# Weights split ahead of their stage get buffers and a schedule of their own, and the first norm's gain moves from the weights to the rows

## The chip, the cores and the metric

The kernel runs on one core of a Trainium2 chip. The time is device microseconds of one execution; a lower one is better. All figures of the trace come from one profiled execution of the kernel before.

## What is computed

Two layers on 512 rows of 1024 values, all float32. The first, a gated short convolution, is the part that the change touches:

```python
h = rmsnorm(x, a_norm)                      # (512, 1024)
b, c, u, z = split(h @ a_w_in, 4)           # a_w_in is 1024 x 8192: 64 column tiles of 128
conv = causal 3-tap convolution of c * u    # per column
x = x + (b * conv * silu(z)) @ a_w_out      # a_w_out is 2048 x 1024
```

Then keys and values are computed from the new x (w_kv, two small compression networks), and an attention layer with three branches follows, whose query, gate and output weights are b_w_in and b_w_out; a last rmsnorm ends it. rmsnorm(x, g) is x times the reciprocal root of its mean square, times the vector g.

## The kernel before

Every product is made in three passes: each float32 operand is split into a high part (rounded to the matmul type) and a low part (the rest), and high x high, high x low and low x high are summed in PSUM (`mm3`, line 160). So every weight tile has to be loaded, rounded on ScalarE (line 148) and subtracted on VectorE (line 149) before TensorE can use it.

Class `Stream` (line 97) does that for a list of units of 128 x 1024 values, in order. `load` (line 108) issues a unit's load on SP's queue into one of NRAW = 3 buffers named raw; `split` (line 122) lets GpSimd multiply it by a norm's gain where it has one (line 147), then makes the high and low tiles. `get(i)` (line 155) hands out unit i, after it has asked for loads up to unit i + 4 and splits up to unit i + 2. A raw buffer is free again when its subtraction has ended. The high and low tiles of the projections have three pairs of buffers (pool `wp`), those of a_w_out four (`wop`).

The list `ws` serves the convolution. Lines 210 to 217 write its order: for each pair of column tiles the eight projection units, and two units of a_w_out among them. For each of the 16 column tiles `conv_tile` (line 304) runs four projections of 24 matmuls with 512 columns (products c, u, z, b), with the convolution and the gate on VectorE and ScalarE (lines 312 to 333). In each pair from the second to the seventh, after its second projection, the four `out_tile` calls (line 336) of the pair before come in a burst: 48 matmuls and eight additions to x on VectorE (line 348). The first norm's gain a_norm is multiplied into each of the 64 units of a_w_in on GpSimd (line 248 passes it, columns S_A of the table `sm`).

24 units of the second layer's weights (q, z and o for four groups) are split ahead in this stage, stored as high and low parts to a tensor in memory (w_dram), and loaded ready from there later (line 125). Lines 220 to 232 mix them into the order of `ws`, about one to every two or three units, so that they use the same three raw buffers; their high and low parts go to four tiles vh0, vl0, vh1 and vl1 in turn, from which line 151 stores them, right behind the split. Before the last two pairs `v_unit` (line 353) loads the weights of V, five raws, through the raw buffers too, and multiplies them by their gains on GpSimd (line 361).

The compiler fixes at compile time in which order each engine, and each queue, issues its instructions: by the order of the program and by when it reckons each one ready. At run time each engine keeps that order and waits on semaphores.

At the start four matmuls on zeros (line 264) run while x arrives. Each of four row tiles is then squared and scaled (`norm_tile`, line 266; the scaling is line 270), transposed (line 181) and split; the first two units of a_w_in are split in quarters, the second one's low part on GpSimd, and their products are made in halves as the row tiles become ready (lines 283 to 294).

Of the kernel before, what the change touches and what calls it, by code (L numbers as in the profile page):

```python
# [9 lines left out]
F32 = mybir.dt.float32  # L10
# [15 lines left out]
S_A = 128  # L26
S_END = 136
# [7 lines left out]
Q0, Z0, Q1, Z1 = 3, 1, 7, 3  # L35

# [6 lines left out]
def trunk_kernel(  # L43
# [13 lines left out]
    small: bass.AP,  # L57
    cst: bass.AP,
# [38 lines left out]
    class Stream:  # L97
# [3 lines left out]
        def add(self, src, a, b, gain=None, pool_=None, tag="w", lo=None, parts=1, put=None):  # L101
            self.units.append((src, a, b, gain, pool_, tag, lo or dve, parts, put))
# [19 lines left out]
        def split(self, upto):  # L122
            while self.at < min(upto, len(self.units)):
# [10 lines left out]
                src, a, b, gain, p_, tag, lo, parts, put = self.units[self.at]  # L134
                r = self.raws[self.at]
                if put is not None:
                    hl_ = p_.tile([128, 2, a, b], F32R, name=tag)
                    h, l = hl_[:, 0], hl_[:, 1]
                else:
                    q = p_ or wp  # L140
                    h = q.tile([128, a, b], F32R, name=tag + "h")
                    l = q.tile([128, a, b], F32R, name=tag + "l")
# [7 lines left out]
                if put is not None:  # L150
                    nc.sync.dma_start(put, f(hl_).rearrange("p s a b -> p s (a b)"))
# [36 lines left out]
    def index_of(order, x_):  # L188
        return order.index(x_)
# [3 lines left out]
    wd = kd.tile([6 * G, 128, 2, 1024], F32, name="w_dram")  # L193
    ready = {}

# [10 lines left out]
    if True:  # L206
# [3 lines left out]
        for i in range(NCT // 2):  # L210
# [12 lines left out]
        first, last_ = index_of(order, ("in", 1, 1)), index_of(order, ("in", 1, 2 * (NCT // 2 - 2)))  # L223
        mixed = []
        n = 0
        for i, o in enumerate(order):
            mixed.append(o)
            while n < len(ahead) and i >= first and (i - first) * len(ahead) >= (n + 1) * (last_ - first - 2):
                mixed.append(("ahead", *ahead[n]))
                n += 1  # L230
        assert n == len(ahead)
        order = mixed
        for o in order:
            index[o] = len(ws.units)
            if o[0] == "ahead":
                kind, g, j = o[1:]
# [131 lines left out]
        for i in range(NCT // 2):  # L368
# [608 lines left out]
```

## Time and profile before

| | |
|---|---|
| median of 3 runs | 880.68 us (876.94 to 881.38) |
| the profiled execution | 880.71 us, of which the span from the first to the last instruction is 878.9 us |
| TensorE, matmuls | 833.6 us busy, 95% of the span |
| TensorE, weight loads | 671.1 us, beside the matmuls |
| VectorE, ScalarE, GpSimd | 612.9, 386.2 and 273.5 us busy |

An engine that is not the bound may be idle without cost; busy time is an average over stages that differ. In the rows below PE is TensorE (PEld its weight loads), DVE VectorE, ACT ScalarE, POOL GpSimd and SP the engine that issues most transfers; L149 is line 149 of the kernel before.

### The profile page before, as it was taken

How to read it: one execution, taken by the hardware profiler on the slowest of the kernel's cores; microseconds unless marked ns; L12 is line 12 of the kernel's file. 1: busy time of each engine (PE TensorE's matmuls, PEld its weight loads, DVE VectorE, ACT ScalarE, POOL GpSimd, SP SyncE). 2: the span in 40 equal slices, each digit the busy share in tenths (PEclk: the TensorE clock that was granted, in tenths of full speed). 3: DMA queues.
4: the chain of work that ended last, by engine and by line, in shares of the span. 5: the costliest groups of instructions: out<-in, count | busy, mean ns of one | idle time of the engine just before them, and what ended most of it. 6: DMA issues, size and time to landing. Idle time of an engine off the chain costs nothing.

```text
span 878.9 us, 10999 instructions
## 1 busy us (share of the span) xinstructions
PE 833.6 (95%) x4004; PEld 671.1 (76%) x4004; DVE 612.9 (70%) x1073; ACT 386.2 (44%) x741; POOL 273.5 (31%) x194
## 2 busy tenths in 40 slices
PE   7999998998999989989999998999999999999995
PEld 6888876776868868868887997776777877877883
DVE  6657646567466485775558529856989869877987
ACT  6422321341243223322233324524867557667675
POOL 6526235334324443443322017220023014012002
PEclk9999999999999999989999999999999999999998
DMA  7477587576486676443352002595214235141212
GB/s 240 116 236 213 180 259 211 166 249 205 145 261 204 193 227 215 136 137 96 96 168 72 1 22 81 170 268 209 85 37 120 66 127 144 49 144 53 93 48 96
DMA packets 121014, 128.31 MB, mean 146 GB/s; under 512 B 5376, under 2 KB 104064, under 8 KB 117888
## 3 DMA queue, kind: packets, MB, share of 16 engines
q1 hardware_dynamic: 117392, 122.50, 44.8%
q0 software_dynamic: 2304, 4.20, 2.2%
q10 hardware_dynamic: 1264, 0.92, 0.3%
q8 instruction: 31, 0.51, 0.2%
q14 instruction: 23, 0.19, 0.1%
HBM read 98.24 MB, written 29.36 MB: 145 GB/s over the span
## 4 chain that ended last, share of the span: by engine, by line
PE 39%; DVE 10%; DMA 4%; ACT 4%; POOL 3%; issue 2%; SPq 0%; ACTq 0%; POOLq 0%; DVEq 0%
PE mm L165 14%; PE mm L690 5%; PE mm L612 4%; PE mm L670 4%; PE pt L774 3%; DVE wl L149 2%; PE o L766 2%; PE o L767 2%; PE s L728 2%; DMA raw<-in_w_kv_dram 2%; PE s L729 2%; DMA raw<-in_a_w_in_dram 1%; POOL raw L147 1%; DVE im L494 1%; ACT wh L148 1%
## 5 line engine op out<-in xcount | busy, mean ns | idle before, releaser
L147 POOL TENSOR_TENSOR raw<-raw,sm 128x1024 f32<-128x1024 f32 (+1 forms) x86 | 169.9, 1985 | 232.4 <-DMA raw<-in_a_w_in_dram 143.1
L165 PE MATMUL mm<-hh,wh 128*128 128x512 f32 (+1 forms) x592 | 233.7, 395 | 7.7 <-DVE x L348 7.5
L165 PE MATMUL mm<-hh,wl 128*128 128x512 f32 (+1 forms) x592 | 232.2, 392 | 3.8 <-DVE wl L149 3.8
L165 PE MATMUL mm<-hl,wh 128*128 128x512 f32 (+1 forms) x592 | 232.7, 393 | 0.4 <-DVE hl L184 0.4
L149 DVE TENSOR_TENSOR wl<-raw,wh 128x1024 fp32r<-128x1024 f32 (+1 forms) x82 | 123.0, 1502 | 38.9 <-ACT wh L148 38.4
L148 ACT ACTIVATE wh<-raw 128x1024 fp32r<-128x1024 f32 (+1 forms) x86 | 85.4, 997 | 141.2 <-PE mm L165 73.2
L165 PEld LDWEIGHTS mm<-hh,wh 128*128 128x128 f32 x592 | 112.5, 190 | 36.0 <-DVE x L348 8.3
L165 PEld LDWEIGHTS mm<-hh,wl 128*128 128x128 f32 x592 | 112.3, 190 | 31.6 <-DVE wl L149 5.6
L165 PEld LDWEIGHTS mm<-hl,wh 128*128 128x128 f32 x592 | 112.6, 190 | 25.4 <-DVE hl L184 0.6
L779 DVE TENSOR_TENSOR pl<-pt,ph 128x512 fp32r<-128x512 f32 x80 | 53.8, 683 | 8.9 <-ACT ph L777 8.0
L165 PE MATMUL mm<-woh,yh 128*128 128x512 f32 x128 | 51.2, 400 | 8.1 <-DVE vp L318 4.6
L777 ACT ACTIVATE ph<-pt 128x512 fp32r<-128x512 f32 x80 | 46.6, 591 | 16.3 <-PE pt L774 14.8
L165 PE MATMUL mm<-woh,yl 128*128 128x512 f32 x128 | 51.1, 399 | 2.5 <-DVE yl L332 2.5
L149 DVE TENSOR_TENSOR vl<-raw,vl 128x1024 fp32r<-128x1024 f32 x12 | 20.0, 1669 | 43.3 <-ACT vl L148 43.3
L165 PE MATMUL mm<-wol,yh 128*128 128x512 f32 x128 | 50.2, 392 | 0.0
L737 ACT ACTIVATE P<-P,st 128x512 f32<-128x512 f32 (+1 forms) x64 | 39.0, 610 | 18.3 <-DVE st L736 18.0
L148 ACT ACTIVATE vl<-raw 128x1024 fp32r<-128x1024 f32 x12 | 12.7, 1061 | 76.3 <-POOL raw L147 39.2
L728 PE MATMUL s<-kh,qs 128*128 128x512 f32 (+3 forms) x128 | 42.1, 341 | 3.7 <-DVE st L736 3.2
L348 DVE TENSOR_TENSOR x<-mm,x 128x512 f32<-128x512 f32 x64 | 41.3, 680 | 5.1 <-PE mm L165 5.1
L774 PE MATMUL pt<-cs,P 128*128 128x128 f32 x192 | 42.4, 275 | 0.0
L729 PE MATMUL s<-kl,qs 128*128 128x512 f32 (+3 forms) x128 | 40.2, 328 | 0.0
L736 DVE CUSTOM_DVE_ANT_0 P<-s,causal 128x512 f32<-128x512 f32 (+1 forms) x64 | 34.6, 550 | 7.4 <-PE s L729 6.7
(206 smaller groups left out, 1608.2 us busy)
## 6 DMA issues: line engine op xcount, KB each, us to landing
raw<-in_a_w_in_dram SPq DMA_DIRECT2D x62, 512.0 KB, 4.8
w_dram<-vh SPq DMA_DIRECT2D x12, 1024.0 KB, 5.1
w_dram<-vl SPq DMA_DIRECT2D x12, 1024.0 KB, 6.2
wh<-w_dram SPq DMA_DIRECT2D x24, 512.0 KB, 4.2
wl<-w_dram SPq DMA_DIRECT2D x24, 512.0 KB, 5.0
raw<-in_b_w_in_dram SPq DMA_DIRECT2D x16, 512.0 KB, 6.7
raw<-in_a_w_out_dram SPq DMA_DIRECT2D x16, 512.0 KB, 3.5
raw<-in_w_kv_dram SPq DMA_DIRECT2D x12, 512.0 KB, 4.5
```

What stands on the lines that cost most here:

```text
L147: pool.tensor_mul(r[:, c], r[:, c], gain[:, c, None].to_broadcast([128, w, b]))
L148: act.activation(h[:, c], r[:, c], AF.Copy)
L149: lo.tensor_sub(l[:, c], r[:, c], f(h[:, c]))
L165: pe.matmul(o, lhsT=a, rhs=b, start=(i == 0), stop=(i == n - 1))
L348: dve.tensor_add(o, p, o)
L690: pe.matmul(p, lhsT=a[:, j, ts_], rhs=b, start=(n == 0), stop=(n == 5))
L728: pe.matmul(p[:, :n], lhsT=q, rhs=K[g][0][:, s, :n], start=True, stop=False)
L729: pe.matmul(p[:, :n], lhsT=q, rhs=K[g][1][:, s, :n], start=False, stop=True)
L737: exps.append(lambda: act.activation(P[:, :n], P[:, :n], AF.Exp, bias=self.st[:, 0, i:i + 1], scale=-1.0, accum_out=self.st[:, 1, i:i + 1]))
L774: pe.transpose(p[:, h, :], self.P[h, s][:, kt * 128:(kt + 1) * 128], ident)
L777: act.activation(ph, p, AF.Copy)
L779: subs.append(lambda p=p, ph=ph, pl=pl: dve.tensor_sub(pl, p, f(ph)))
```

## The change

A class `Ahead` takes the 24 units out of `ws`. A unit is loaded straight into the low half of one of the four tiles (vh0, vl0, vh1, vl1), its high part is made in the other half, and the subtraction is made in place. One `tick` n issues the load of unit n + 2, the split of unit n and the store of unit n - 1. After each of the 64 projection steps the loop asks for as many ticks as the share of steps between the fifth (A0) and the 46th (A1) gives. The units' order becomes q, z, o within each group and half. `ready_or` and `KV_AHEAD = False` leave the units of the stage after as they were.

The units of a_w_in have no gain any more. The vector a_norm is loaded as one row, a product of a column of ones with it spreads it over all 128 rows in two PSUM banks, and the first norm's scaling takes it as a second factor, half a row at a time. Of the four matmuls on zeros one goes.

```diff
-S_A = 128
-S_END = 136
+S_END = 128
...
+A0, A1 = 5, 46
+KV_AHEAD = False
...
-                if put is not None:
-                    hl_ = p_.tile([128, 2, a, b], F32R, name=tag)
-                    h, l = hl_[:, 0], hl_[:, 1]
...
-                if put is not None:
-                    nc.sync.dma_start(put, f(hl_).rearrange("p s a b -> p s (a b)"))
...
+    class Ahead:
+        def __init__(self):
+            self.units, self.slots, self.at, self.out = [], {}, 0, 0
+
+        def add(self, key, src, a, b, gain=None):
+            ready[key] = (wd[len(self.units)], a, b)
+            self.units.append((src, a, b, gain))
+
+        def load(self, n):
+            if n < len(self.units):
+                src, a, b, _ = self.units[n]
+                r = vwp.tile([128, 2, a, b], F32, name=("vh0", "vl0", "vh1", "vl1")[n % 4])
+                nc.sync.dma_start(r[:, 1], src)
+                self.slots[n] = r
+
+        def tick(self):
+
+            n = self.at
+            if n == 0:
+                self.load(0)
+                self.load(1)
+            self.load(n + 2)
+            if n < len(self.units):
+                _, a, b, gain = self.units[n]
+                r = self.slots[n]
+                if gain is not None:
+                    pool.tensor_mul(r[:, 1], r[:, 1], gain[:, :, None].to_broadcast([128, a, b]))
+                act.activation(r[:, 0].bitcast(F32R), r[:, 1], AF.Copy)
+                dve.tensor_sub(r[:, 1].bitcast(F32R), r[:, 1], r[:, 0])
+            if 0 < n <= len(self.units):
+                nc.sync.dma_start(wd[n - 1], self.slots.pop(n - 1).rearrange("p s a b -> p s (a b)"))
+            self.at += 1
+
+        def upto(self, share):
+            while self.at < share * (len(self.units) + 1):
+                self.tick()
...
-        ahead = [("q", 0, 0), ("q", 0, 1)] + [
-            (k, g_, j) for g in range(G) for k, g_ in (("z", g), ("o", g), ("q", g + 1)) if g_ < G for j in range(2)
-        ]
...
-                ws.add(row_units(a_w_in, o[1] * CD + o[2] * 128), KC, 128, sm[:, S_A:S_A + KC], lo=pool if len(ws.units) == 1 else dve, parts=4 if len(ws.units) < 2 else 1)
+            if o[0] == "in":
+                ws.add(row_units(a_w_in, o[1] * CD + o[2] * 128), KC, 128, None, lo=pool if len(ws.units) == 1 else dve, parts=4 if len(ws.units) < 2 else 1)
...
+        grow = wop.tile([1, D], F32, name="woh", padded_shape=[128, D])
+        ones = wop.tile([1, 128], F32, name="wol", padded_shape=[128, D])
+        pool.memset(ones, 1.0)
+        nc.scalar.dma_start(grow, a_norm)
         nc.scalar.dma_start(sm, small)
...
-        for _ in range(4):
+        gain = []
+        for d in range(2):
+            p = psum.tile([128, 512], F32, name="mm")
+            pe.matmul(p, lhsT=ones, rhs=grow[:, d * 512:(d + 1) * 512], start=True, stop=True)
+            gain.append(p)
+        for _ in range(3):
...
-            dve.tensor_scalar(xn, x2[:, t, :], r, None, op0=OP.mult)
+            if gain is None:
+                dve.tensor_scalar(xn, x2[:, t, :], r, None, op0=OP.mult)
+            else:
+                for d in range(2):
+                    c = slice(d * 512, d * 512 + 512)
+                    dve.scalar_tensor_tensor(xn[:, c], x2[:, t, c], r, gain[d], op0=OP.mult, op1=OP.mult)
...
+        for g in range(G):
+            for j in range(2):
+                ah.add(("q", g, j), row_units(b_w_in, g * 256 + j * 128), KC, 128, bq)
+                ah.add(("z", g, j), row_units(b_w_in, 1072 + g * 256 + j * 128), KC, 128, gb)
+                ah.add(("o", g, j), b_w_out[(2 * g + j) * 128:(2 * g + j + 1) * 128, :].rearrange("p (a b) -> p a b", a=1), 1, 1024)
+        seen = 0
         for i in range(NCT // 2):
...
                 for _ in conv_tile(c):
                     n += 1
+                    seen += 1
+                    ah.upto(min(1.0, max(0.0, (seen - A0) / (A1 - A0))))
```

## Rows read from the trace of the kernel before

**Rows 1.** The page: busy us, share of the span and instructions per engine

```profile
PE 833.6 (95%) x4004; PEld 671.1 (76%) x4004; DVE 612.9 (70%) x1073; ACT 386.2 (44%) x741; POOL 273.5 (31%) x194
```

**Rows 2.** Table by stage: length; PE, PEld, DVE, ACT, POOL busy (instructions); clock; DMA; GB/s

```profile
26.50:120.00 93.50, 93.50 (x404) 75.52 (x403) 60.39 (x57) 30.29 (x34) 38.95 (x22) 1.00 0.65 200
120.00:400.00 280.00, 262.85 (x1095) 206.88 (x1095) 178.13 (x173) 84.81 (x96) 116.00 (x65) 0.98 0.65 197
400.00:460.00 60.00, 60.00 (x259) 48.28 (x258) 35.41 (x34) 17.78 (x21) 16.73 (x11) 1.00 0.41 120
```

**Rows 3.** TensorE's waits, 120 to 400 us: total, times, longest

```profile
PE mm L165 <- DVE x L348: 7.5, 5, 2.9
PE mm L165 <- DVE vp L318: 4.6, 3, 2.8
PE mm L165 <- ACT yh L331: 3.4, 4, 1.5
PE mm L165 <- DVE yl L332: 1.6, 3, 0.6
```

**Rows 4.** Chain that ended last, in order of time: start, length, what

```profile
338.81 7.94 DMA raw<-in_a_w_in_dram
...
346.89 1.91 POOL raw L147
...
348.82 1.07 ACT wh L148
...
349.91 2.01 DVE wl L149
```

**Rows 5.** DMA issues, 120 to 400 us: count, KB each, median us to landing

```profile
raw<-in_a_w_in_dram SPq DMA_DIRECT2D x39, 512.0 KB, 4.9
...
w_dram<-vl SPq DMA_DIRECT2D x9, 1024.0 KB, 6.1
raw<-in_b_w_in_dram SPq DMA_DIRECT2D x11, 512.0 KB, 6.7
raw<-in_a_w_out_dram SPq DMA_DIRECT2D x8, 512.0 KB, 3.8
raw<-in_b_w_out_dram SPq DMA_DIRECT2D x6, 512.0 KB, 5.8
```

**Rows 6.** Groups by line, 120 to 400 us: busy us, mean ns, idle before and releasers

```profile
L147 POOL TENSOR_TENSOR raw<-raw,sm 128x1024 f32<-128x1024 f32 x45 | 94.8, 2115 | 124.9 <-DMA raw<-in_a_w_in_dram 91.6 <-DMA raw<-in_b_w_in_dram 22.7 <-DVE cv L322 6.6
...
L149 DVE TENSOR_TENSOR wl<-raw,wh 128x1024 fp32r<-128x1024 f32 x36 | 55.3, 1535 | 23.5 <-ACT wh L148 23.4
...
L149 DVE TENSOR_TENSOR vl<-raw,vl 128x1024 fp32r<-128x1024 f32 x9 | 14.1, 1564 | 38.2 <-ACT vl L148 38.2
...
L318 DVE TENSOR_TENSOR vp<-mm,cc 128x512 f32<-128x512 f32 x9 | 6.1, 681 | 0.4 <-PE mm L165 0.4
```

**Rows 7.** The start: two small loads, timeline rows of TensorE, durations of the norm's scaling

```profile
sm<-in_small_dram ACTq DMA_DIRECT2D x1, 68.0 KB, 5.1
cs<-in_cst_dram ACTq DMA_DIRECT2D x1, 64.0 KB, 4.0
...
1.23 5.49 PE L264 MATMUL mm<-causal 128*128 128x384 f32 x8 [1.23 <-POOL causal L89]
...
7.10 1.09 PE L181 MATMUL mm<-cs,xn 128*128 128x128 f32 x8 [0.38 <-DVE xn L270]
...
14.91 1.94 DVE L270 TENSOR_SCALAR xn<-x,stat 128x1024 f32<-128x1024 f32 x1
...
17.82 0.37 PE L165 MATMUL mm<-hh,wh 128*128 128x256 f32 x1
...
L270 DVE TENSOR_SCALAR xn<-x,stat x4: 753/1029/1937, 6.3 to 14.9; 128x1024 f32<-128x1024 f32 x4
```

**Rows 8.** SP's waits, 120 to 400 us: total, times, longest

```profile
SPq L151 <- DVE vh L149: 27.0, 6, 6.2
...
SPq L151 <- DVE vl L149: 16.2, 4, 6.7
```

More of the change, by code (lines that the diff above doesn't have):

```diff
@@ L57, in trunk_kernel @@
     small: bass.AP,
+    a_norm: bass.AP,
     cst: bass.AP,
@@ L133, in split @@
                     continue
-                src, a, b, gain, p_, tag, lo, parts, put = self.units[self.at]
+                src, a, b, gain, p_, tag, lo, parts = self.units[self.at]
                 r = self.raws[self.at]
-                if put is not None:
-                    hl_ = p_.tile([128, 2, a, b], F32R, name=tag)
-                    h, l = hl_[:, 0], hl_[:, 1]
[L139 to L142, printed above, removed]
+                q = p_ or wp
+                h = q.tile([128, a, b], F32R, name=tag + "h")
+                l = q.tile([128, a, b], F32R, name=tag + "l")
                 w = a // parts
@@ L186, in trunk_kernel @@
     ws = Stream()
-    def index_of(order, x_):
-        return order.index(x_)
     kd = ctx.enter_context(tc.tile_pool(name="kd", bufs=1, space=bass.MemoryType.DRAM))
     k_dram = kd.tile([2, 2, G * HD, T], F32, name="k_dram")
-    wd = kd.tile([6 * G, 128, 2, 1024], F32, name="w_dram")
+    NB = 6 * G + 16
+    wd = kd.tile([NB, 128, 2, 1024], F32, name="w_dram")
     ready = {}
+    class Ahead:
[29 more added lines that the diff above has]
+                self.tick()
     vw_stack = ExitStack()
@@ L367, in trunk_kernel @@
         gkv, gb = sm[:, S_KV:S_KV + KC], sm[:, S_B:S_B + KC]
+        ah = Ahead()
+        if KV_AHEAD:
+            for st, w1, c0 in (("k", w1k, 0), ("v", w1v, 256)):
+                for j in range(2):
+                    ah.add(("c" + st, j), row_units(w_kv, c0 + j * 128), KC, 128, gkv)
+                for j in range(4):
+                    ah.add(("w1" + st, j), row_units(w1, 0, 4, 256, j * 512), 4, 256)
+            for s in range(2):
+                for j in range(2):
+                    ah.add(("rk", s, j), row_units(w_kv, 512 + 512 * s + j * 128), KC, 128, gkv)
+        for g in range(G):
+            for j in range(2):
+                ah.add(("q", g, j), row_units(b_w_in, g * 256 + j * 128), KC, 128, bq)
+                ah.add(("z", g, j), row_units(b_w_in, 1072 + g * 256 + j * 128), KC, 128, gb)
+                ah.add(("o", g, j), b_w_out[(2 * g + j) * 128:(2 * g + j + 1) * 128, :].rearrange("p (a b) -> p a b", a=1), 1, 1024)
+        seen = 0
         for i in range(NCT // 2):
@@ L391, in add, with ready_or @@
         bs.add(*a, **k)
+    def ready_or(key, *a):
+        if key in ready:
+            bi[key] = len(bs.units)
+            bs.add_ready(*ready[key])
+        else:
+            add(key, *a)
     def add_c(st, j):
-        add(("c" + st, j), row_units(w_kv, (0 if st == "k" else 256) + j * 128), KC, 128, gkv)
+        ready_or(("c" + st, j), row_units(w_kv, (0 if st == "k" else 256) + j * 128), KC, 128, gkv)
     def add_w1(st, j):
-        add(("w1" + st, j), row_units(w1k if st == "k" else w1v, 0, 4, 256, j * 512), 4, 256)
+        ready_or(("w1" + st, j), row_units(w1k if st == "k" else w1v, 0, 4, 256, j * 512), 4, 256)
     def add_rk(s, j):
-        add(("rk", s, j), row_units(w_kv, 512 + 512 * s + j * 128), KC, 128, gkv)
+        ready_or(("rk", s, j), row_units(w_kv, 512 + 512 * s + j * 128), KC, 128, gkv)
     for i, st in enumerate(ORDER):
@@ L415, in add_b @@
             bi[k, g, j] = len(bs.units)
-            bs.add_ready(ready[k, g, j], *((1, 1024) if k == "o" else (KC, 128)))
+            bs.add_ready(*ready[k, g, j])
     add_b("q", 0)
@@ L949 @@
     conv = a["a_conv_w"].reshape(3, NCT, 128).transpose(2, 1, 0).reshape(128, 48)
[L950 removed]
+    small = np.concatenate([cols(a["kv_norm"]), cols(a["b_norm"]), conv] + pos(a["cmp_pos_k"]) + pos(a["cmp_pos_v"]), axis=1)
     arrays = {
```

39 lines of the change are left out of this document (8 added, 31 removed).

## The prediction

> **What bounds the kernel now.** The page comes first: TensorE is busy 95% of the span [rows 1], so time can be won only where it stands still. A table by stage says where that is [rows 2]. From 400 to 460 us TensorE runs without a gap: 259 matmuls in 60.00 us, 0.2317 us each, the floor used below. From 26.5 to 120 us it holds that pace too (404 x 0.2317 = 93.6 against 93.50). From 120 to 400 us it does not: 1095 x 0.2317 = 253.7 us of matmuls took 280.00, so **26.3 us** are lost. Of these 17.15 are plain idle time (280.00 - 262.85); the rest are matmuls stretched at restarts and by the clock, whose mean granted value is 0.98 there. What follows 460 us is not touched by the change.
>
> The list of waits names VectorE results as the last releasers (x, vp, yh by way of ScalarE, yl) [rows 3], but that is not the cause. The chain of waits shows it [rows 4]: a load of 7.94 us, GpSimd's multiply 1.91, ScalarE's copy 1.07, VectorE's subtraction 2.01, and only then the next load into the buffer that was freed. The reader should see a ring: three raw buffers, each held from the issue of its load to its VectorE subtraction. From 120 to 400 us 69 raws went through them (39 + 11 + 6 + 8 [rows 5], and five of the V weights, lines 371 and 372), one per 280 / 69 = 4.06 us, so a buffer was held some 12.2 us. By rows a pass costs 4.9 to 6.7 us (load) [rows 5], 2.1 (multiply) [rows 6], 1.07 (copy) [rows 4] and 1.54 (subtraction) [rows 6], 9.6 to 11.4 before any queueing: **the ring is full**. 17 of the 69 (11 + 6) are units split ahead, which no matmul of this stage uses. VectorE works in order, so a late raw holds up everything behind its subtraction, and those are the results that rows 3 name. From 400 to 460 us, with the multiply still there but neither units split ahead nor additions to x, nothing waits.
>
> **The change, part by part.**
> *Units split ahead leave the ring.* 24 raws less in the whole stage, 17 of them in the stretch that loses. 52 stay, in what would be 253.7 us: one per 4.88 us, 14.6 us for a buffer. The work itself (24 loads, copies, subtractions and stores, 16 multiplies on GpSimd) stays beside the matmuls; VectorE is busy only 178.13 of 280 us there [rows 2].
>
> *GpSimd's multiply goes from all 64 units of a_w_in.* 39 multiplies of some 2.1 us [rows 5, 6] go from the stretch, and a pass of the ring shrinks to 4.9 + 1.07 + 1.54 = 7.5 us plus queueing. Against 14.6 us that leaves half the ring idle.
>
> *Loads two ticks ahead, stores one tick behind.* The 25 ticks are spread over 41 projection steps. A step is 24 matmuls, 5.56 us, or more with an out burst, so a tick comes every 41 / 25 = 1.64 steps, 9 us, more where a burst falls between, and two in neighbouring steps are 5.56 us apart. A load thus has 11 us or more to land (5.8 to 6.7 needed), and a buffer's store (6.1) is issued a tick ahead of the load that reuses the buffer, so it has landed by then, or is at worst 0.6 us late [rows 5]. What SP issues behind that load is a raw needed two or more units (11 us) later: 0.
>
> *What the stretch keeps.* Five out bursts, and the five raws of the V weights, whose multiplies still pass the ring. Bounds for what is lost after the change: 0 (the stretch from 26.5 to 120 us held a burst of 48 matmuls from 71 us on and lost nothing) and 13.5 (the waits for vp, yh and yl and the two longest for x: 4.6 + 3.4 + 1.6 + 2.9 + about 1 [rows 3], all of VectorE's order and none of the ring's). I take **4**, near the lower end, because the nearest rows are the unlost stretches. Gain: 26.3 - 4 = **22.3 us**.
>
> *The start.* Two products of a row of ones with the norm weights stand ahead of the warm-up matmuls, of which one goes. They need a 4 KB load queued second on ScalarE: its neighbours took 4.0 and 5.1 us to land [rows 7], so it is there at 1.2 + 4.0..5.1 = 5.2 to 6.3 us. The warm-ups took 5.49 us for 8 half-products of 384 columns [rows 7], 0.69 each; four of 512 columns take 3.7 us at that rate and perhaps half of it if TensorE is faster by then. The first normalised row tile, ready at 7.1 us before (its transposes start there [rows 7]), gets its scale between 7.1 and 10.0 and is then two operations of 0.68 to 0.74 (a 512-column VectorE operation on PSUM took 681 ns [rows 6], 0.74 is my margin for the scalar; no row shows this one) in place of 0.75 to 1.94 [rows 7]. So the first tile comes 1.4 to 4.4 us later. The steady matmuls begin at 17.82 us, behind the fourth tile's normalisation at 14.91 [rows 7]; in between, the eight quarter multiplies that paced the first weights are gone. Bounds: -2.6 (the fourth scaling falls from 1.94 us to 1.4, and a multiply of 2.1 ahead of the weights goes [rows 6, 7]) and +4.4. I take **+1.5**, below the middle, as the queue that waits there was paced by the very multiplies removed.
>
> On that operation, rows first: the old one took 753 ns at best, 1029 at the median [rows 7]. The Trainium skill, "VectorE: DVE Perf Modes", section "The perf-mode tier table", puts an fp32 single-source operation in SBUF at double rate, and any with a second tensor or a PSUM operand at single rate, which speaks against this edit. By it each tile costs 1.38 - 0.75 = 0.6 us more (an estimate from its fixed cost and clock), at most 2.5 for four, and the forecast would be 861.
>
> Everything else (the shorter table of small vectors, a ones tile, the new bookkeeping) is off the path: 0.
>
> **Sum** against the profiled execution, 880.71 us (span 878.9; the median of the three runs is 880.68, the same): 880.71 - 22.3 + 1.5 = **860 us**.
>
> **Rivals.**
> *A. VectorE's order was the cause, the ring only half.* For: rows 3 name VectorE alone, the V weights still use the ring, and the out bursts still want 8 additions of 0.68 us among the splits. Against: the burst at 71 us cost nothing. Price: all 13.5 us of those waits stay: 880.7 - (26.3 - 13.5) + 3 = 871.
> *B. It does not take the wait away:* the compile-time order of instructions puts the split-ahead copies and subtractions ahead of nearer work, so ScalarE and VectorE still stand behind a load. For: VectorE waited 38.2 us for ScalarE's copy of such units [rows 6]. Against: the data now lands at least a tick ahead of its copy. Time: 880.7 - 3 + 1.5 = 879.
> *C. Slower: SP.* It issues in order. A store waits at SP for its subtraction, and a load waits for a store to have landed; raws of the ring stand behind both. Stores already held SP 43.2 us (27.0 + 16.2) from 120 to 400 us [rows 8], for 17 units 2.5 each. Were each load to wait out its buffer's store of 6.1 us [rows 5] as well, SP would stand 8.6 us per unit, and 12.8 with the longest wait of 6.7. The ring spares (14.6 - 7.5) / 3 = 2.4 us per raw, 7.3 per unit split ahead (52 / 17 = 3.06 raws); it turns slower than before by 4.4 us from 9.1 per unit on (17 x 1.8 = 31 us lost against 26.3). Midway between 8.6 and 12.8, at 10.7: 17 x 3.4 = 58 lost, 880.7 - 26.3 + 58 + 1.5 = **914**. Against: a store has at least 5.56 us before its load.
>
> **Chances.** The forecast (853 to 867) 0.69, A 0.18, B 0.08, C 0.05. What a measurement here can tell from no change is about 0.5%, 4.4 us. Faster by more than that (below 876.3): forecast, A: 0.87; within it: B, 0.08; slower: C, 0.05. The range reaches down to a stretch that loses nothing at the lower bound of the start (880.7 - 26.3 - 2.6 = 851.8) and up to A with the whole cost of the start (880.7 - 12.8 + 4.4 = 872.3), each with a little for the stages behind, whose order the compiler makes anew: 851 to 874.
>
> **What would show it.** Right: from 120 us to the end of the convolution's projections no TensorE wait above a microsecond and 0.232 us per matmul; chains without a_w_in loads; no GpSimd multiply of a_w_in; the x additions of the last burst some 22 us earlier than now; steady matmuls from 17 to 22 us on. Wrong: waits for vp, x or yl as long as now (A), ScalarE waiting for the split-ahead loads (B), SP's raws issued behind stores with loads late (C), or steady matmuls only after 22 us.

## The result, and the profile after

The changed kernel took 867.93 us (median of 4 runs, 863.0 to 869.48) against 880.96 us for the kernel before on the same chip: ratio 0.985, 95% interval 0.981 to 0.989. Its profiled execution took 866.97 us, with a span of 865.2 us (before: 880.71 and 878.9). The forecast was 860.0 with a range of 851 to 874: the direction and the range were right, and the time came out eight microseconds above the forecast.

In the views below line 161 is the projections' and out tiles' matmul (165 before), 177 the transposes, 147 the stream's subtraction, 145 its multiply on GpSimd, 203, 217 and 221 the load, the multiply and the store of class Ahead, 284 the first norm's squares, 291 its scaling, 353 the subtraction that makes yl, and 319 a copy of constants that only the attention layer uses. The page first:

```profile
PE 829.5 (96%) x4006; PEld 674.8 (78%) x4006; DVE 575.6 (67%) x1077; ACT 386.2 (45%) x741; POOL 136.0 (16%) x125
```

GpSimd's busy time halved (273.5 us in [rows 1]). The table by stage, columns as in [rows 2]:

```profile
26.50:120.00 93.50, 93.50 (x436) 77.48 (x435) 61.32 (x66) 37.26 (x41) 17.15 (x13) 1.00 0.94 314
120.00:400.00 280.00, 280.00 (x1211) 227.81 (x1211) 152.03 (x174) 81.72 (x95) 22.33 (x21) 1.00 0.50 159
400.00:460.00 60.00, 57.78 (x243) 46.48 (x243) 38.02 (x39) 20.01 (x24) 9.39 (x4) 0.97 0.40 120
440.00:460.00 20.00, 17.78 (x71) 14.06 (x70) 16.41 (x17) 6.84 (x9) 6.66 (x3) 0.91 0.33 98
```

From 120 to 400 us there are 1211 matmuls where 1095 were, at 0.2312 us each: the 26.3 us are gone to the last one. The next stretch loses in their place: from 400 to 460 us 243 matmuls ran where 259 did, 16 x 0.2317 = 3.7 us. TensorE's waits from 26 to 460 us are one row (line, releaser; total, times, longest), where [rows 3] had four:

```profile
PE mm L161 <- DVE yl L353: 2.2, 1, 2.2
```

The timeline of the same place (start, length, engine, line) shows why. GpSimd is multiplying w_kv weights when VectorE comes to the subtraction yl. That takes 2.38 us, where it takes 0.68 alone, and ends half a microsecond after the multiply does (452.03 and 451.49 us); only then can TensorE go on:

```profile
449.22 2.27 POOL L145 TENSOR_TENSOR raw<-raw,sm 128x1024 f32<-128x1024 f32 x1 [4.83 <-DMA raw<-in_w_kv_dram]
...
449.65 2.38 DVE L353 TENSOR_TENSOR yl<-cv,yh 128x512 fp32r<-128x512 f32 x1
...
452.09 0.50 PE L161 MATMUL mm<-woh,yl 128*128 128x512 f32 x1 [2.22 <-DVE yl L353]
```

In the kernel before, TensorE waited 0.93 us for yl at the same point of the program (470.69 us).

The start is the other place that got worse. Timeline, to be read against [rows 7]:

```profile
4.90 3.74 PE L276 MATMUL mm<-woh,wol 1*128 1x512 f32 x4 [4.90 <-DMA woh<-in_a_norm_dram]
8.57 4.21 PE L280 MATMUL mm<-causal 128*128 128x384 f32 x6
12.57 2.27 PE L177 MATMUL mm<-cs,xn 128*128 128x128 f32 x16
...
15.50 1.08 ACT L284 ACTIVATE xn<-x 128x1024 f32<-128x1024 f32 x1
...
18.69 0.23 DVE L319 COPY causal<-raw 128x128 f32<-128x128 f32 x1 [2.00 <-DMA raw<-in_cst_dram]
...
19.48 1.90 POOL L217 TENSOR_TENSOR vh<-vh,bq 128x1024 f32<-128x1024 f32 x1 [6.36 <-DMA vh<-in_b_w_in_dram]
...
20.42 2.04 DVE L147 TENSOR_TENSOR wl<-raw,wh 128x1024 fp32r<-128x1024 f32 x1
...
22.38 1.40 DVE L291 SCALAR_TENSOR_TENSOR xn<-x,stat,mm 128x512 f32<-128x512 f32 x2
...
24.66 0.56 PE L161 MATMUL mm<-hh,wh 128*128 128x256 f32 x1
```

TensorE stands until the gain row lands at 4.90 us, and the matmuls on zeros, which used to fill that time, now come behind the products. The transposes start at 12.57 us (7.10 before), the steady matmuls at 24.66 (17.82 before).

The steady matmuls wait for the fourth row tile, which is scaled at 22.38 us in place of 14.91, 7.5 later. Part of that comes by way of ScalarE, which squares the third tile only behind the evictions of the first transposes, 4.0 us later than in the kernel before:

```profile
11.51 1.05 ACT L268 ACTIVATE xn<-x 128x1024 f32<-128x1024 f32 x1
```

The rest is in VectorE's order. It stands until 18.69 us for a load of constants (line 319), although ScalarE's roots for the third and fourth tile were there at 18.07, and then makes the subtraction of a weight tile ahead of the fourth scaling. That subtraction takes 2.04 us in place of 1.22, because a GpSimd multiply of a unit split ahead is running.

The groups by shape of the first 60 us give the price in work: 111 matmuls of 512 columns where 144 were, with 96 of 256 in both. 33 x 0.2317 = **7.6 us**. These are the rows of one of the three products, of the kernel before and of the changed one:

```profile
L165 PE MATMUL mm<-hh,wl 128*128 128x512 f32 x48 | 18.8, 392 | 0.0
```

```profile
L161 PE MATMUL mm<-hh,wl 128*128 128x512 f32 x37 | 14.6, 395 | 0.0
```

The rows of the V weights' tile and of the keys' tile date the end of the convolution and the first scores (name, count; min/median/max ns, first to last start us). Of the kernel before:

```profile
L165 PE MATMUL mm<-vh,hh x64: 278/302/367, 490.2 to 516.6; 128*128 128x256 f32 x32, 128*128 128x304 f32 x32
...
L728 PE MATMUL s<-kh,qs x128: 221/337/500, 597.7 to 850.4; 128*128 128x512 f32 x32, 128*128 128x384 f32 x32, 128*128 128x256 f32 x32, 128*128 128x128 f32 x32
```

Of the changed kernel:

```profile
L161 PE MATMUL mm<-vh,hh x64: 278/302/367, 473.2 to 499.6; 128*128 128x256 f32 x32, 128*128 128x304 f32 x32
...
L774 PE MATMUL s<-kh,qs x128: 221/337/502, 583.4 to 836.3; 128*128 128x512 f32 x32, 128*128 128x384 f32 x32, 128*128 128x256 f32 x32, 128*128 128x128 f32 x32
```

So 17.0 us are won at the end of the convolution, 14.3 at the first scores, 13.7 at the end of the span.

One thing in the profile contradicts the text of the change. The units split ahead don't keep their ticks. The load's and the store's rows (durations ns, first and last start us):

```profile
L203 SPq DMA_DIRECT2D vh<-in_b_w_in_dram x8: 367/480/625, 11.7 to 160.3; - x8
```

```profile
L221 SPq DMA_DIRECT2D w_dram<-vh x12: 320/476/2135, 26.1 to 182.4; - x12
L221 SPq DMA_DIRECT2D w_dram<-vl x12: 338/504/1548, 28.5 to 187.8; - x12
```

All 24 units have had their stores issued by 188 us instead of being spread to about 290: nothing but a free slot holds a unit back, and the compile-time order put each in as soon as it had one. The DMA share of 0.94 from 26.5 to 120 us (0.65 before) is theirs. SP did wait for stores then, from 26 to 210 us:

```profile
SPq L203 <- DMA w_dram<-vh: 18.2, 4, 7.1
...
SPq L203 <- DMA w_dram<-vl: 5.1, 3, 2.6
```

This is the wait of rival C, and no matmul of that stretch waited for it.

### The profile page after: what moved, and what is told of

Its sections match the earlier page's. It is cut to its first block, busy times and chain, and to the rows that moved or that the text cites. A ratio compares the mean times of both kernels' runs of the same rounds, so it can differ in the third digit from the quotient of the medians.

```text
span 865.2 us, 10915 instructions
## 1 busy us (share of the span) xinstructions
PE 829.5 (96%) x4006; PEld 674.8 (78%) x4006; DVE 575.6 (67%) x1077; ACT 386.2 (45%) x741; POOL 136.0 (16%) x125
## 4 chain that ended last, share of the span: by engine, by line
PE 79%; DVE 10%; POOL 3%; ACT 3%; issue 3%; DMA 2%; ACTq 0%; DVEq 0%; POOLq 0%
PE mm L161 54%; PE mm L736 5%; PE mm L658 5%; PE mm L716 4%; PE pt L820 3%; PE o L813 2%; PE o L812 2%; PE s L774 2%; DVE wl L147 2%; PE s L775 2%; POOL im L540 1%; DVE im L540 1%; DMA raw<-in_cst_dram 1%; DVE iml L550 1%; PE mm L177 1%
## 5 line engine op out<-in xcount | busy, mean ns | idle before, releaser
L147 DVE TENSOR_TENSOR wl<-raw,wh 128x1024 fp32r<-128x1024 f32 (+1 forms) x82 | 103.0, 1260 | 68.0 <-ACT wh L146 67.8
L823 ACT ACTIVATE ph<-pt 128x512 fp32r<-128x512 f32 x80 | 46.5, 591 | 16.0 <-PE pt L820 14.6
L782 DVE CUSTOM_DVE_ANT_0 P<-s,causal 128x512 f32<-128x512 f32 (+1 forms) x64 | 34.6, 551 | 7.4 <-PE s L775 6.7
L783 ACT ACTIVATE Pb<-Pb,st 128x384 f32<-128x384 f32 (+1 forms) x64 | 32.1, 502 | 13.8 <-DVE st L782 13.6
L813 PE MATMUL o<-pl,vt 128*128 128x512 f32 x80 | 33.8, 423 | 2.0 <-DVE pl L825 2.0
```

Source lines behind the costliest of these rows:

```text
L147: lo.tensor_sub(l[:, c], r[:, c], f(h[:, c]))
L783: exps.append(lambda: act.activation(P[:, :n], P[:, :n], AF.Exp, bias=self.st[:, 0, i:i + 1], scale=-1.0, accum_out=self.st[:, 1, i:i + 1]))
L813: pe.matmul(O, lhsT=w, rhs=pl, start=False, stop=False)
L823: act.activation(ph, p, AF.Copy)
```

## The experiments

All ratios are against the kernel before, run beside each kernel on its chip. "Lost" in a stretch is its length less the number of matmuls times 0.2317 us.

### Which of the two edits carries the gain

**Own slots alone (e1).** Class Ahead as in the change; the gain stays on the weights, the start as before.

```diff
-                ws.add(row_units(a_w_in, o[1] * CD + o[2] * 128), KC, 128, None, lo=pool if len(ws.units) == 1 else dve, parts=4 if len(ws.units) < 2 else 1)
+                ws.add(row_units(a_w_in, o[1] * CD + o[2] * 128), KC, 128, sm[:, S_A:S_A + KC], lo=pool if len(ws.units) == 1 else dve, parts=4 if len(ws.units) < 2 else 1)
...
-        xs[0] = norm_tile(0, gain)
+        xs[0] = norm_tile(0)
```

> Only the units split ahead move: the gain stays on the weights of a_w_in, multiplied on GpSimd, and the start is that of the kernel before. If the ring of three raw buffers was full (52 raws with a pass of 9.6 to 11.4 us against 14.6 us per buffer), the stretch from 120 to 400 us loses 0 to 4 us in place of 26.3, the steady matmuls start at 17.8 us, and the time is 856 to 862 us, below the changed kernel's 868. If GpSimd's multiply is what kept VectorE late, the stretch still loses 15 us or more: 870 to 880 us.

Measured: 876.52 us, ratio 0.995 (0.993 to 0.997), a miss. By the table by stage most of the loss has only moved to the front, where the 24 units stand one behind the other (stores from 29 to 206 us):

```profile
26.50:215.00 188.50, 178.01 (x738) 140.18 (x737) 139.18 (x127) 66.35 (x76) 93.19 (x49) 0.97 0.87 287
215.00:360.00 145.00, 145.00 (x626) 117.16 (x625) 82.13 (x80) 38.58 (x45) 42.21 (x27) 1.00 0.33 98
```

Lost up to 215 us: 188.5 - 738 x 0.2317 = 17.5 us. From 215 to 360 us, with the multiplies of a_w_in still there but no unit split ahead, nothing is lost; from 360 to 400, beside the V weights, 2.7 us (161 matmuls).

**The norm edit alone (e2).** The 24 units stay in the ring of three raw buffers, at their old places in the order. Two lines of the edit, against the changed kernel:

```diff
+                mixed.append(("ahead", *ahead[n]))
...
-                    ah.upto(min(1.0, max(0.0, (seen - A0) / (A1 - A0))))
```

> Only the gain moves: the units split ahead stay in the ring, 69 raws in the stretch, 11.0 us per buffer at TensorE's pace against a pass of 7.5 us plus queueing. The ring theory expects 5 to 13 us lost in the stretch in place of 26.3 and a start that is 7 us later, as in the changed kernel: 868 to 876 us. If the units split ahead alone filled the ring: 26 us still lost and the late start on top, 886 to 890 us.

Measured: 866.75 us, ratio 0.986 (0.983 to 0.988), which is the whole change. 69 raws still pass the ring, and yet:

```profile
120.00:400.00 280.00, 279.01 (x1206) 226.68 (x1205) 156.67 (x183) 89.54 (x103) 33.98 (x27) 1.00 0.65 204
```

```profile
L149 DVE TENSOR_TENSOR wl<-raw,wh 128x1024 fp32r<-128x1024 f32 x40 | 48.8, 1220 | 19.1 <-ACT wh L148 19.1
```

Taking the multiply away is enough. Beside it, with three raw buffers, the own slots bring nothing that can be measured. The subtraction fell from 1535 ns [rows 6] to 1220: the multiply had cost VectorE time too, and not only the raw buffer.

### What the multiply cost: a longer pass, or VectorE's time

Both experiments start from the norm-only kernel. **e5** gives GpSimd its work back without making the copy wait for it (the product goes to a tile that nothing uses); **e6** lengthens the pass without arithmetic on any engine, by a transfer that writes one value again. The edit of e5:

```diff
+                    if a == KC and put is None and parts == 1 and gain is None:
+                        for e in range(2):
+                            g8 = sm[:, S_B + 4 * e:S_B + 4 * e + 4, None].to_broadcast([128, 4, b])
+                            pool.tensor_mul(scr, r[:, 4 * e:4 * e + 4], g8)
                     act.activation(h[:, c], r[:, c], AF.Copy)
```

> The norm-only kernel (866.75 us: gain in the rows, units split ahead still in the ring of three raw buffers) with two GpSimd multiplies of half a tile added for every a_w_in unit behind the first two. They read the raw tile and write a scratch tile that nothing uses, so GpSimd works as long as before the change (about 62 x 2.1 us) beside ScalarE's copy and VectorE's subtraction, but the copy does not wait for it. Contention theory (the loss of 26 us from 120 to 400 us came from GpSimd working beside VectorE): subtractions at 1.5 to 2.0 us again and the loss comes back, 20 to 26 us, total 885 to 893. Pass-length theory (it came from the 2.1 us that the multiply added to each raw buffer's pass): the multiply runs beside copy and subtraction (1.07 + 1.5 us), the pass grows by 0 to 0.5 us, total 866 to 871.

Measured: 877.42 us, ratio 0.998 (0.996 to 1.001): 10.7 us more than the norm-only kernel, between the two expectations.

```profile
120.00:400.00 280.00, 272.52 (x1164) 219.13 (x1163) 177.74 (x181) 87.76 (x100) 142.80 (x109) 0.99 0.64 202
```

```profile
L151 POOL TENSOR_TENSOR scr<-raw,sm 128x512 f32<-128x512 f32 x82 | 109.1, 1331 | 84.6 <-DMA raw<-in_a_w_in_dram 80.5
L153 DVE TENSOR_TENSOR wl<-raw,wh 128x1024 fp32r<-128x1024 f32 x40 | 61.0, 1527 | 12.9 <-ACT wh L152 10.9 <-PE mm L169 2.0
```

Lost: 280 - 1164 x 0.2317 = 10.3 us, and the subtraction is back at 1527 ns. GpSimd's two reads of a raw take 2 x 1.33 us beside ScalarE's 1.05 and VectorE's 1.53, so they hold the buffer hardly longer than these do: SP waited for them in 6 of its loads, 6.4 us in all. Company on GpSimd alone costs about 10 us here. Its price before the change may have differed: e5's multiplies are of half a tile, so each holds VectorE up for a shorter time, but GpSimd is busy for longer (142.80 us against 116.00). And the slower subtraction is itself part of a raw's pass, so the two causes cannot be parted entirely.

The edit of e6:

```diff
+                if a == KC and put is None and parts == 1 and gain is None:
+                    nc.gpsimd.dma_start(r[0:1, 0, 0:1], src[0:1, 0, 0:1])
                 for i in range(parts):
```

> The norm-only kernel (866.75 us) with a transfer of one number added behind every a_w_in load, on GpSimd's queue, into the same raw buffer (it writes the value that is there). It does no arithmetic on any engine, but ScalarE's copy now waits for load and small transfer one after the other, so that each pass of the ring is longer by one small transfer, estimated at 2 us or more (no row shows one). Pass-length theory: the loss from 120 to 400 us comes back, by 15 to 26 us, total 880 to 893. Contention theory: VectorE's subtractions stay near 1.2 us and nothing is lost, total 866 to 870.

Measured: 904.81 us, ratio 1.030 (1.026 to 1.033), beyond the expected 893.

```profile
120.00:400.00 280.00, 253.79 (x1059) 203.12 (x1057) 146.39 (x160) 81.54 (x93) 53.47 (x60) 0.95 0.59 190
```

```profile
raw<-in_a_w_in_dram POOLq DMA_DIRECT2D x35, 0.0 KB, 3.7
```

```profile
L145 POOL DMA_DIRECT2D raw<-in_a_w_in_dram x35 | 18.7, 535 | 146.5 <-DMA raw<-in_a_w_in_dram 110.8 <-DVE yl L348 14.5 <-DVE cv L337 9.3
```

The small transfer took 3.7 us and 0.54 to issue, twice the multiply's 2.1: the pass became 4.5 (the raw load's median in that run) + 0.5 + 3.7 + 1.05 + 1.4 = 11.2 us, as long as before the change (9.6 to 11.4 by the prediction), and 280 - 1059 x 0.2317 = 34.6 us are lost. The wl subtraction averaged 1399 ns, those of the units split ahead 1222 to 1224, so little of this is VectorE's time. The edit has a side effect: from 120 to 400 us SP, which issues the loads in order, waited 69.3 us for transfers of a_w_in into raw, a wait that the kernel before does not have. So not all of the 34.6 us need be the buffers' own. That a ring too short for its passes costs this much is shown without the side effect by the runs with two buffers below; e5 adds a second mechanism that the prediction did not have. By these runs some 10 of the 26.3 us are GpSimd's company and the other 16 or so the longer pass; the second figure is a difference and was not measured by itself.

### What the own slots are worth

Two raw buffers in place of three, in the changed kernel (e11) and in the norm-only one (e12):

```diff
-NRAW = 3
+NRAW = 2
```

> The changed kernel with two raw buffers in place of three. Ring theory: 52 raws from 120 to 400 us leave 254 x 2 / 52 = 9.8 us per buffer against a pass of 7.5 us and queueing, so 0 to 6 us are lost: 868 to 874. If the ring never mattered, 866 to 870 here and no loss in the norm-only kernel with two buffers either.

Measured: 891.6 us, ratio 1.012 (1.009 to 1.014).

```profile
120.00:400.00 280.00, 275.23 (x1177) 223.10 (x1176) 148.24 (x171) 81.86 (x94) 21.47 (x21) 0.99 0.50 157
...
520.00:580.00 60.00, 49.55 (x244) 40.47 (x243) 41.23 (x44) 22.48 (x29) 20.83 (x17) 0.91 0.47 145
```

The stretch lost 280 - 1177 x 0.2317 = 7.3 us, just over the 0 to 6 expected. The total was missed, because the same buffers serve the stage of keys and values: from the first V-weight matmul (480.3 us) to the first score (600.3) it took 120.0 us, 9.8 more than in the changed kernel.

> The norm-only kernel (units split ahead still in the ring) with two raw buffers. Ring theory: 69 raws leave 254 x 2 / 69 = 7.4 us per buffer, less than a pass of 7.5 us and queueing, so the ring is full again and 15 to 40 us are lost: 882 to 907. If the own slots of the change do nothing for the ring, the same as the changed kernel with two buffers.

Measured: 918.27 us, ratio 1.041 (1.037 to 1.045).

```profile
120.00:400.00 280.00, 257.65 (x1072) 203.71 (x1071) 154.37 (x170) 85.25 (x95) 37.99 (x27) 0.97 0.65 197
```

Lost in the stretch: 31.6 us, within the 15 to 40 expected; the total is above the expected 907, by the later stage again (120.6 us from the first V-weight matmul to the first score, 110.7 with three buffers). The convolution ended at 507.3 us (first V-weight matmul) against 480.3 with own slots. So the slots are worth 27 us where the ring is short, and nothing that can be measured where a third buffer covers it. The prediction's "half the ring idle" was too generous: with two buffers, 9.8 us per pass in place of 14.6, the 7.5 us of a pass and its queueing no longer fitted everywhere.

**Pacing (e7).** Own slots alone as above, but each load waits for a transfer of one number from the convolution tile of its tick into its slot.

```diff
+                nc.sync.dma_start(r[0:1, 1, 0, 0:1], mark[0][0:1, 0:1])
                 nc.sync.dma_start(r[:, 1], src)
```

> The ahead-only kernel (876.52 us: own slots, gain still multiplied into the weights by GpSimd, start as before) with each load of a unit split ahead held back by a transfer of one number from the newest convolution tile of its tick into its slot, so that the ticks hold at run time: 24 units over 41 projection steps, some 55 to 290 us, in place of 12 to 188 us. Bunching theory (the 21 us that ahead-only lost before 215 us were the price of 24 units in a row beside the GpSimd multiplies): the loss falls to 0 to 8 us, total 856 to 864. Rival (GpSimd's multiplies and the ring alone cost it, wherever the units stand): the loss only spreads over 50 to 300 us and total stays at 872 to 880. A third outcome: the small transfers hold SP's queue and the raws behind it come late, total above 880.

Measured: 867.55 us, ratio 0.988 (0.984 to 0.992), 6 to 9 us less than without pacing (6 by the ratios, 9 by the medians), yet above the expected 856 to 864.

```profile
L207 SPq DMA_DIRECT2D vh<-in_b_w_in_dram x8: 367/410/1468, 57.5 to 289.0; - x8
```

```profile
120.00:400.00 280.00, 272.69 (x1154) 219.03 (x1153) 189.94 (x178) 85.96 (x98) 123.72 (x66) 0.98 0.63 195
```

The ticks now hold (loads from 57.5 to 300 us), and 280 - 1154 x 0.2317 = 12.6 us are lost with GpSimd's multiplies still there. Half of the 26.3 us was had by own slots too, where the units kept their distance, and the whole of it only without the multiply. That 12.6 us stay while 17 raws are gone fits the 10.3 us of company on GpSimd in e5; that they are the same microseconds was not shown.

### The start

**The matmuls on zeros first (e3)**, then the two products.

```diff
+        for _ in range(3):
+            p = psum.tile([128, 512], F32, name="mm")
+            pe.matmul(p[:, :T - 128], lhsT=causal[:, :128], rhs=causal[:, :T - 128], start=True, stop=True)
         gain = []
...
-        for _ in range(3):
-            p = psum.tile([128, 512], F32, name="mm")
-            pe.matmul(p[:, :T - 128], lhsT=causal[:, :128], rhs=causal[:, :T - 128], start=True, stop=True)
```

> The changed kernel with the three matmuls on zeros written ahead of the two products that spread the gain, nothing else. If the late start (first transposes at 12.6 us in place of 7.1, steady matmuls at 24.7 in place of 17.8) comes from TensorE's order, matmuls on zeros that stand behind a load, then the transposes start at 8.5 to 9.5 us, the steady matmuls at 18.5 to 21, and the time is 860 to 864 us. If it comes from the load and from the two operations that replace one, the start stays above 23 us and the time at 866 to 870.

Measured: 868.56 us, ratio 0.988 (0.986 to 0.990). The start did come forward:

```profile
9.07 3.14 PE L177 MATMUL mm<-cs,xn 128*128 128x128 f32 x12
...
20.75 0.37 PE L161 MATMUL mm<-hh,wh 128*128 128x256 f32 x1
```

It was lost again. From 120 to 400 us 1194 matmuls ran in place of 1211 (3.9 us), and from the first V-weight matmul at 472.0 us to the first score at 584.8 it took 112.8 us, 2.6 more than in the changed kernel. Only the compile-time order differs there; which of its waits cost this was not looked into.

**No matmuls on zeros (e4).** They compute nothing that is used.

```diff
-        for _ in range(3):
-            p = psum.tile([128, 512], F32, name="mm")
-            pe.matmul(p[:, :T - 128], lhsT=causal[:, :128], rhs=causal[:, :T - 128], start=True, stop=True)
```

> The changed kernel without the three matmuls on zeros (they enter no result). If the transposes stood behind them, the first comes at 10 to 10.5 us, two operations after the products end at 8.6, and the steady matmuls at 20.5 to 22.5 us, if a lower clock does not take it back: 862 to 866 us. If the matmuls on zeros cost nothing there, the time stays at 868.

Measured: 865.14 us, ratio 0.984 (0.981 to 0.986). The first transposes came at 9.67 us, but the steady matmuls only at 24.49. From 20 to 40 us:

```profile
20.00:40.00 20.00, 18.25 (x110) 16.88 (x111) 16.35 (x19) 9.01 (x11) 5.36 (x4) 0.83 0.81 271
```

The granted clock is 0.83 there (0.91 in the changed kernel, 1.00 before): TensorE, which had been busy only 11.13 us in the first 20 (13.41 in the changed kernel, 15.44 before), spent part of this stretch at 1.2 of its 2.4 GHz. So the zero matmuls are not what holds the steady matmuls back. As in the changed kernel it is VectorE's order:

```profile
18.67 0.23 DVE L316 COPY causal<-raw 128x128 f32<-128x128 f32 x1 [2.53 <-DMA raw<-in_cst_dram]
```

Here too it stands for the load of constants, and a subtraction of 1.70 us, beside a GpSimd multiply, comes ahead of the fourth scaling (22.02 us). In e3 the compile-time order has that copy behind all four scalings, at 22.53 us, and the fourth scaling starts at 18.81. In the norm-only kernel (e2), with no unit split ahead in the start, the copy stands ahead again, the subtraction takes 1.20 us, and the fourth scaling comes at 20.91, the steady matmuls at 22.84. No run moved the copy alone.

**The row spread by its transfer (e9).** The gain is loaded to all 128 partitions, so TensorE has no part in it, four matmuls on zeros come first as before the change, and the scaling is one operation on SBUF.

```diff
-        grow = wop.tile([1, D], F32, name="woh", padded_shape=[128, D])
-        ones = wop.tile([1, 128], F32, name="wol", padded_shape=[128, D])
-        nc.scalar.dma_start(grow, a_norm)
+        grow = wop.tile([128, D], F32, name="woh")
+        nc.scalar.dma_start(grow, a_norm.to_broadcast([128, D]))
...
-        gain = []
-        for d in range(2):
-            p = psum.tile([128, 512], F32, name="mm")
-            pe.matmul(p, lhsT=ones, rhs=grow[:, d * 512:(d + 1) * 512], start=True, stop=True)
-            gain.append(p)
-        for _ in range(3):
+        gain = grow
+        for _ in range(4):
...
-                for d in range(2):
-                    c = slice(d * 512, d * 512 + 512)
-                    dve.scalar_tensor_tensor(xn[:, c], x2[:, t, c], r, gain[d], op0=OP.mult, op1=OP.mult)
+                dve.scalar_tensor_tensor(xn, x2[:, t, :], r, gain, op0=OP.mult, op1=OP.mult)
```

> The changed kernel (867.93 us) with the gain row spread over the 128 partitions by its transfer (512 KB into one of the a_w_out tiles) in place of two products on TensorE, four zero matmuls as before, and the scaling as one operation of 1024 columns out of SBUF. Theory (the start lost 6.8 us because the products wait for a load and the zero matmuls stand behind them): first transposes at 7.5 to 9.5 us in place of 12.57, steady matmuls at 18 to 21 us in place of 24.66, total 861 to 865. Rival 1: the wider transfer lands only at 8 to 10 us or holds up x, total 866 to 870. Rival 2: as with the zero matmuls put first (steady at 20.75 us, no gain in total), what the start wins is lost behind it, total 866 to 869.

Measured: 860.17 us (859.59 to 861.98), ratio 0.977 (0.975 to 0.978), better than both kernels.

```profile
10.61 3.44 PE L177 MATMUL mm<-cs,xn 128*128 128x128 f32 x16 [3.90 <-DVE xn L283]
...
22.28 0.37 PE L161 MATMUL mm<-hh,wh 128*128 128x256 f32 x1
```

```profile
18.32 1.56 DVE L283 SCALAR_TENSOR_TENSOR xn<-x,stat,woh 128x1024 f32<-128x1024 f32 x1
```

```profile
woh<-in_a_norm_dram ACTq DMA_DIRECT2D x1, 512.0 KB, 6.9
```

Neither time was hit: the wide transfer takes 6.9 us and the transposes wait for it until 10.61 (expected 7.5 to 9.5), the steady matmuls start at 22.28 (18 to 21). The copy of constants stands behind the scalings here (24.29 us). TensorE stood idle for 3.90 us before the transposes, and its granted clock was 0.84 in the first 20 us (1.00 in the changed kernel). Still, 125 matmuls of 512 columns are done by 60 us (111 in the changed kernel, 144 before), 14 x 0.2317 = 3.2 us sooner. The V-weight matmuls start at 467.9 us, 5.3 sooner than in the changed kernel, and from there to the first score (575.2) it took 107.3 us in place of 110.2. No view here ties that last 2.9 us to the edit; the order of the instructions in that stage is another one.

**The same with pacing (e10).**

```diff
+                nc.sync.dma_start(r[0:1, 1, 0, 0:1], mark[0][0:1, 0:1])
                 nc.sync.dma_start(r[:, 1], src)
```

> The same with each load of a unit split ahead held back by a transfer of one number from the newest convolution tile of its tick, so that none of them is in the first 40 us. Theory: GpSimd's multiplies and the loads of the split-ahead units no longer stand beside the fourth row tile, steady matmuls 1 to 3 us earlier than without it, and from 26 to 440 us nothing is lost either way: 859 to 863. Rival: the pacing only moves the multiplies beside the out bursts, 1 to 5 us lost there: 864 to 868.

Measured: 858.67 us (857.63 to 860.57), ratio 0.975 (0.973 to 0.976). It cannot be told from the one above. The ahead loads start at 61.9 us, DMA from 26 to 120 us falls from 0.92 to 0.66, and the steady matmuls begin at 22.61 us, no sooner than with the units in the start. In this start they are not what is waited for.

### The stage behind: w_kv and w1 split ahead too (e8)

```diff
-KV_AHEAD = False
+KV_AHEAD = True
```

> The changed kernel (867.93 us) with the 16 units of the stage after (w_kv, w1) split ahead as well. Theory: the stall at 440 to 460 us (17.78 of 20 us busy, w_kv multiplies on GpSimd beside VectorE) and the waits of the key and value stage go, worth 2 to 5 us: 863 to 866. Rival: 16 more units, 8 of them with a GpSimd multiply, beside the convolution bring back waits there and more stores on the DMA queues, 868 to 873.

Measured: 875.52 us, ratio 0.995 (0.993 to 0.997): 7.6 us slower than the changed kernel, worse than either expectation.

```profile
120.00:400.00 280.00, 275.75 (x1185) 222.00 (x1184) 172.32 (x190) 95.56 (x110) 46.56 (x31) 1.00 0.75 249
...
440.00:460.00 20.00, 20.00 (x89) 16.31 (x88) 9.97 (x14) 3.68 (x6) 0.00 (x0) 1.00 0.61 195
...
540.00:560.00 20.00, 15.87 (x85) 13.56 (x83) 4.27 (x8) 2.43 (x6) 0.00 (x0) 0.83 0.92 331
```

```profile
PE mm L161 <- DMA wh<-w_dram: 2.3, 2, 1.1
PE mm L565 <- DMA wl<-w_dram: 2.1, 2, 1.3
PE mm L565 <- DMA wh<-w_dram: 2.0, 1, 2.0
```

The stall at 452 us is gone, as the theory said. But the rival's waits came back in the convolution: from 120 to 400 us 280 - 1185 x 0.2317 = 5.4 us are lost, and its end is 2.5 us later (first V-weight matmul at 475.7 us). From there to the first score it took 116.0 us, 5.8 more than in the changed kernel. A unit split ahead comes back as two tiles of 512 KB where the raw one has 512 KB in all, and the stage of keys and values consumes units fast. Its DMA share from 540 to 560 us is 0.92, TensorE waits for the loads themselves, and its clock falls to 0.83 while it does.

## Why the prediction was right, and where its size was off

*The ring.* Right in what it gave: the 26.3 us were read as a stretch that the change frees, and it lost nothing after (the residual of 4 was too careful). Right in the mechanism, as far as it goes: a ring of two loses 31.6 us without own slots and 7.3 with them (e12, e11), and a longer pass brings 34.6 us of loss, part of it perhaps by SP's waits (e6). Incomplete in two points. The step that put the multiply into the pass and nowhere else missed its price on VectorE, about 10 us (e5), although [rows 6] showed 1535 ns for the subtraction. A subtraction that comes while GpSimd multiplies does not end before the multiply has. And the two edits do not share the gain: the norm edit alone has all of it (e2), own slots alone have a quarter to a third (ratio 0.995 against 0.985; e1). The part that the prediction put first, units leaving the ring, was not needed for this result. Left open is why the same ring lost nothing from 26.5 to 120 us: 24 raws went through it in 93.5 us there, 11.7 us for a buffer, where TensorE's pace behind it asks for 11.0.

*Ticks.* The steps that counted "a tick every 9 us", "11 us or more to land" and "a store has 5.56 us" took the program's order for the order on the chip. The units ran from 11.7 to 188 us, bunched. Behind the start it cost the changed kernel nothing from 26.5 to 400 us, with no multiply of a_w_in beside them; in e1 it cost 6 to 9 us, the difference that pacing makes (e7).

*The start* is the term that failed: +1.5 (bounds -2.6 to +4.4) was 7.6. By the prediction's own signs this counts against it: steady matmuls at 24.66 us are "only after 22 us", and the last addition to x came 17.0 us earlier (472.6 in place of 489.6), not 22. The step that lets the scale be there "between 7.1 and 10.0" was met: the products ended at 8.6 and the first scaling started at 8.75. But the first tile's lateness was carried on one for one, and the two products were thought to sit ahead of zero matmuls that nothing needs. In fact these stayed behind the products in TensorE's order and held it for 4.21 us; without them the first transposes come at 9.67 us, 2.9 earlier (e4). And the fourth tile, which sets the steady matmuls, was to be paced as before or better: it came at 22.38 us, behind ScalarE's later squares, a copy that waits for constants, and a subtraction held up for 0.8 us by a GpSimd multiply of a unit split ahead, which the ticks should have kept out of the start. How much each of the three cost was not tested one by one.

*The scaling.* It took 1.40 us per row tile as predicted (0.70 for each half). By the Trainium skill, "VectorE: DVE Perf Modes", section "The perf-mode tier table", it would be 1.38 (an estimate from its fixed cost and clock), and the trace agrees; one operation of 1024 columns out of SBUF took 1.28 (e9).

*What was called untouched.* Two losses lie behind the convolution's last pairs: 3.7 us at 440 to 460 us, where a w_kv multiply meets the last gate's subtraction, and 3.3 us after the V weights (17.0 to 13.7). The first is read from the timeline, and it goes where the w_kv units go (e8, which takes their subtractions away with their multiplies). The second is in no view a single wait: the stage takes 107.5 us before, 110.2 after, 107.3 in e9 and 112.8 in e3, with the same instructions in another compile-time order. Which of its orders is good, and why, stays open.

The balance against 860 us: start +6.1 (7.6 - 1.5), residual -4, stall at 452 us +3.7, later stages +3.3, and -2.0 that the convolution's end gained beyond these terms (0.9 of it the stall at 470 us of the kernel before, the rest unexplained): 867.1, against 866.97 in the profiled execution. The three terms that cost add up to 13.1 us, and that the other two took 6.0 of it back is luck.

*Rivals.* A was wrong: the waits for vp, yh, yl and x went altogether. B was wrong for the whole change and nearly right for own slots alone (876.5 against its 879), but whether by its mechanism is open: VectorE waited 38.6 us there for ScalarE's copies of units split ahead (26.5 to 215 us), as B said, and also in the changed kernel (37.3 us from 26 to 460 us), where it cost nothing. C's wait was there, 23.3 us of it up to 210 us, and harmless.

## What to carry to other kernels

A helper that scales a tile in place can cost twice: its own time in every buffer's pass, which is slack of the ring, and the time of the engine beside it that has to wait for it. Fold the factor into the smaller operand, and spread it by a transfer rather than by products that TensorE has to wait for. A schedule written as ticks holds only if something waits for the tick: look at first and last start of the rows before you reckon with distances.

## What the runs showed of the hardware

VectorE and GpSimd hold each other up, and whichever starts first goes on. In the kernel before, VectorE made 126 subtractions of 128 x 1024 float32. Of these, 88 started with no GpSimd multiply or subtraction running and took 1.22 us on average, also where one started during them. The other 38 started under a running one, and 37 of these ended 1.08 us after it ended, however much of it had been left (0.2 to 1.8 us). In the rows of the start above it is the same: the multiply ends at 21.38 us, the subtraction that came at 20.42 ends at 22.46. A GpSimd multiply of 128 x 1024 took 1.90 us where VectorE was idle at its start (38) and 2.28 at the median where it was not (54). The Trainium skill, "SBUF — State Buffer", section "Who interferes with whom", has the two engines share a port pair under an exclusive lock; the traces agree, with these numbers.

A transfer of one number from memory into SBUF took 3.7 us on GpSimd's queue (e6), not far from loads of 512 KB, which took 3.4 to 6.7 us there. One row spread to 128 partitions, 512 KB in all, took 6.9 us at the start beside other loads (e9). The stores of units split ahead landed in 7.7 us at 314 GB/s from 26.5 to 120 us, against 6.6 and 6.9 us at 200 GB/s in the kernel before.
